# Layer 0's mixer stage in another order: the first products, the 64-row products of the recurrent mixer, and the additions of a sum of squares

## The chip, the cores and the metric

The kernel runs on one core of one Trainium2 chip. The metric is the device time of one execution in microseconds, median of several runs. A profiled execution gives the trace from which all rows below come.

## What is computed

A two-layer encoder trunk works on 1024 new frames of one stream and 64 frames of a running stream: 1088 columns in all (T), of model width 1024. Layer 0, the only one that the change touches, has two mixers behind one normalisation: a short gated convolution and a gated recurrent mixer (GLA) of four heads, 64 key and 128 value rows each. Per chunk of 64 frames:

```python
h = rms_norm(x, norm_mix[0])
... = split(h @ w_in_ab)
log_a = log_sigmoid(gk_low @ gk_w2 + gk_b) / 16
b = cumsum(log_a);  q_e = q * exp(b);  k_e = k * exp(-b)
att = where(causal, q_e @ k_e.T, 0)
o = att @ v + q_e @ S
S = exp(b_last) * S + (k * exp(b_last - b)).T @ v
o = rms_norm(o, onorm) * silu(g)
```

After it come the output projection with a residual and a SwiGLU FFN. Layer 1 is softmax attention over a band of chunks, with its own FFN.

## The kernel before

All activations stand transposed, features on the partitions and frames on the columns, in three column groups of 384, 384 and 320 (`GROUPS`, L24). Weights and activations are split into a high and a low part of a shorter float type (`hi`, `lo`), and each product is made of three: hi·hi, hi·lo, lo·hi (`chain`, L241). One `gemm` (L253) is three chains of 24 products, one for each group. The normalisation is not applied to the input: the sum of squares `RS` over the 1024 features goes through a product with ones, and 1/rms is multiplied in when a product leaves PSUM.

Layer 0's mixer stage, the first 415 us, is in this order:

- **First products** (L573 to L597). For each group and each of 8 row tiles: `hi` is the input times a gain (on ACT, or on DVE for odd tiles, L582), `lo` the rest (DVE, L585), the square is added into `RS[g]` by GpSimd (L590), and eight products go to three banks, `pg` (gate), `pk` (keys) and `pq` (queries) of the first pair of heads. Behind each group a `tail` (L557) is started, which makes 1/rms, the low-rank gate input `gkl` (L567), the exponentials of the gates (`gate_exps`, L370) and the scaled keys and queries.
- **v**, two GEMMs (L599, L600), whose results are turned to frames-on-partitions by `to_tokens` (L359).
- **The recurrent mixer** `gla_mix` (L447), beside the GEMMs of the output gate (`gla_gate`, L435) and of the second pair's k, q, v; then again for the second pair of heads beside the next gate GEMMs and the convolution's.

In `gla_mix` a pair of heads stands on the two halves of the 128 partitions. For each chunk a state product `kv` for each head takes 64 rows: the upper half for an even chunk, the lower half for an odd one. For each group and head there is then a score product `at` over 128-frame tiles (64 rows, those of the head), a mask on DVE, and an output product `po`: for each tile attention times v over 128 rows, then the two chunks' states over the head's 64 rows. A product with ones over its squares follows (`ss`, L510), for the norm.

TensorE's order is written by the kernel itself (`PEOrder`, L41): the main line issues GEMM products, each of which spends its modelled time, and side jobs (Python generators) are resumed when their time is due. `yield 2500.0` means that the job goes on 2500 ns of modelled TensorE time later. The other engines' order is a scheduler's. The places in question:

```python
                    mm(kv[:, hh * P:(hh + 1) * P], d["kd"][r, t, :], d["v"][hh][r, t, :], True, True)
...
                yield 1000.0
...
                    mm(at[0:w, i, 0:w], d["E2"][r, cols], d["E1"][r, cols], True, True)
...
                yield 2500.0
                po = gps.tile([P, 512], F32, name="ao")
                for i in range(ntl):
...
                nc.gpsimd.tensor_tensor(RS[g], RS[g], x, op=ALU.add)
```

ACT evaluates silu from one table of functions, and logarithm and exponential from another; an `ACT_TABLE_LOAD` stands in its order wherever the table changes. The two silus of a pair (L441) wait for the gate GEMMs.

Of the kernel before, what the change touches and what calls it, by code (L numbers as in the profile page):

```python
# [10 lines left out]
F32 = mybir.dt.float32  # L11
# [7 lines left out]
P = 128  # L19
# [112 lines left out]
def trunk_kernel(  # L132
# [60 lines left out]
    def mm(out, lhsT, rhs, start, stop):  # L193
        pe.matmul(out, lhsT, rhs, start=start, stop=stop)  # L194
        n = rhs.free_size()
        order.spend(max(214.0, n / 0.6) if lhsT.dtype == F32 else max(107.0, n / 2.4))
# [22 lines left out]
    def fetch():  # L219
        if wpos[0] == len(wlist):  # L220
            return
        src, nk = wlist[wpos[0]]
        wpos[0] += 1
        raw = wpool.tile([P, KT, P], F32, name="wraw", bufs=1)
        sp.dma_start(raw[:, 0:nk, :], src)
        hi = wpool.tile([P, KT, P], F32R, name="whi")
        lo = wpool.tile([P, KT, P], F32R, name="wlo")
        with tc.high_priority(offset=-100):
            act.copy(hi[:, 0:nk, :], raw[:, 0:nk, :])  # L229
            for a, b in ((0, nk),) if cur["sub"] is dve else ((0, nk // 2), (nk // 2, nk)):  # L230
                cur["sub"].tensor_tensor(lo[:, a:b, :], raw[:, a:b, :], hi[:, a:b, :].bitcast(F32), op=ALU.subtract)  # L231
        order.use("act", nk * P)
        order.use("dve" if cur["sub"] is dve else "pool", nk * P)
        wready.append((hi, lo))
# [6 lines left out]
    def chain(w, acts, g, evac):  # L241
        hi, lo = w
        c0, c1 = GROUPS[g]
        nk = len(acts)
        ps = mm_tile()
        v = ps[:, 0:c1 - c0]
        for k, (ah, al) in enumerate(acts):
            mm(v, hi[:, k, :], ah[:, c0:c1], k == 0, False)
            mm(v, hi[:, k, :], al[:, c0:c1], False, False)
            mm(v, lo[:, k, :], ah[:, c0:c1], False, k == nk - 1)  # L250
        evac(g, c0, c1, v)

    def gemm(acts, evac):  # L253

        w = next_weights()
        for g in range(len(GROUPS)):
            chain(w, acts, g, evac)
# [188 lines left out]

    def gla_mix(pr, d):  # L447

        S = None
        for g, (c0, c1) in enumerate(GROUPS):  # L450
            n = c1 - c0
            nch = n // CH
            ntl = (n + P - 1) // P
            states = []
            for cl in range(nch):
                c = c0 // CH + cl
                t, cc = c // 2, c % 2
                kv = gps.tile([P, 512], F32, name="kv")
                r = slice(cc * CH, (cc + 1) * CH)
                for hh in range(2):  # L460
                    mm(kv[:, hh * P:(hh + 1) * P], d["kd"][r, t, :], d["v"][hh][r, t, :], True, True)
                if c == TP // CH:
                    sp.dma_start(o_gla[0, pr], S)
                    S = G1.tile([P, P], F32, name="S", bufs=7)
                    sp.dma_start(S, glas[pr])
                states.append(S)
                Sn = G1.tile([P, P], F32, name="S", bufs=7)
                for hh in range(2):
                    r = slice(hh * CH, (hh + 1) * CH)
                    if S is None:  # L470
                        dve.tensor_copy(Sn[r, :], kv[r, hh * P:(hh + 1) * P])
                    else:
                        dve.scalar_tensor_tensor(Sn[r, :], S[r, :], d["E4"][r, c:c + 1],
                                                 kv[r, hh * P:(hh + 1) * P], op0=ALU.mult, op1=ALU.add)
                S = Sn
                yield 1000.0
            if g == 2:
                sp.dma_start(o_gla[1, pr], S)
            for hh in range(2):
                r = slice(hh * CH, (hh + 1) * CH)  # L480
                at = gps.tile([P, 4, P], F32, name="ao")
                for i in range(ntl):
                    w = min(P, n - i * P)
                    cols = slice(c0 + i * P, c0 + i * P + w)
                    mm(at[0:w, i, 0:w], d["E2"][r, cols], d["E1"][r, cols], True, True)
                am = attm[attc[0] % 2]
                attc[0] += 1
                full = n // P
                for i in range(full):
                    dve.copy_predicated(am[:, i, :], cmask, at[:, i, :])  # L490
                if n % P:
                    dve.copy_predicated(am[0:CH, full, 0:CH], cmask[0:CH, 0:CH], at[0:CH, full, 0:CH])
                yield 2500.0
                po = gps.tile([P, 512], F32, name="ao")
                for i in range(ntl):
                    w = min(P, n - i * P)
                    mm(po[:, i * P:i * P + w], d["v"][hh][:, 3 * g + i, :], am[:, i, 0:w], True, False)
                    for cc in range(w // CH):
                        st = states[2 * i + cc]
                        if st is None:  # L500
                            continue
                        k0 = i * P + cc * CH
                        mm(po[:, k0:k0 + CH], st[r, :], d["E1"][r, c0 + k0:c0 + k0 + CH],
                           False, cc == w // CH - 1)
                o_sb = gtmp()[:, 0:n]
                act.copy(o_sb, po[:, 0:n])
                sq = gtmp()[:, 0:n]
                act.activation(sq, o_sb, AF.Square)
                yield 3500.0
                ss = tr_tile()[:, 0:n]  # L510
                mm(ss, ones, sq, True, True)
                z = gtmp()[:, 0:n]
                rsqrt_newton(ss, n, float(P), z, sq, 1)
                dve.scalar_tensor_tensor(o_sb, o_sb, on, z, op0=ALU.mult, op1=ALU.mult)
                while not d["gate"]:
                    yield 1000.0
                dve.tensor_tensor(o_sb, o_sb, d["sg"][hh][:, c0:c1], op=ALU.mult)
                yh, yl = YB[2 * pr + hh]
                split(o_sb, yh[:, c0:c1], yl[:, c0:c1])
# [36 lines left out]

    def tail(g, c0, c1, pg, pk, pq):  # L557
        n = c1 - c0
        yield 3000.0
        ss = tr_tile()[:, 0:n]  # L560
        mm(ss, ones, RS[g], True, True)
        t = scratch()
        rsqrt_newton(ss, n, float(KT * P), RS[g], t[:, 0:n], 1)
        gl = gkl[:, c0:c1]
        act.copy(gl, pg[32:48, :])
        dve.tensor_tensor(gl, pg[0:16, :], gl, op=ALU.add)
        dve.tensor_tensor(gl, gl, RS[g][0:16, :], op=ALU.mult)  # L567
        yield 5800.0
        gate_exps(0, dd[0], g, c0, c1)
        ek(g, c0, c1, pk)  # L570
        eq(g, c0, c1, pq)

    for g, (c0, c1) in enumerate(GROUPS):  # L573
        n = c1 - c0
        pg, pk, pq = [t[:, 0:n] for t in (mm_tile(), gps.tile([P, 512], F32, name="kv"),
                                          gps.tile([P, 512], F32, name="ao"))]
        for k in range(KT):
            x = xs[k][:, c0:c1]
            hi, lo = xg[k][0][:, c0:c1], xg[k][1][:, c0:c1]
            gcol = gain[:, 0, k:k + 1]  # L580
            if k % 2:
                dve.tensor_scalar(hi, x, gcol, None, op0=ALU.mult)  # L582
            else:
                act.activation(hi, x, AF.Copy, scale=gcol)
            dve.scalar_tensor_tensor(lo, x, gcol, hi.bitcast(F32), op0=ALU.mult, op1=ALU.subtract)  # L585
            if k == 0:
                act.activation(RS[g], x, AF.Square)
            else:
                act.activation(x, x, AF.Square)
                nc.gpsimd.tensor_tensor(RS[g], RS[g], x, op=ALU.add)  # L590
            first, end = k == 0, k == KT - 1
            for ps, wh, wl in ((pg, gw, None), (pk, khi, klo), (pq, qhi, qlo)):
                mm(ps, wh[:, k, :], hi, first, False)
                mm(ps, wh[:, k, :], lo, False, end and wl is None)
                if wl is not None:
                    mm(ps, wl[:, k, :], hi, False, end)
        order.start(tail(g, c0, c1, pg, pk, pq))  # L597
    fetch()
    gemm(xg, ev0)  # L599
    gemm(xg, ev1)  # L600
    order.flush()
    zero_tails(dd[1])
    order.start(gla_mix(0, dd[0]))

    def gates1():
        for g, (c0, c1) in enumerate(GROUPS):
            gate_exps(1, dd[1], g, c0, c1)
            yield 3000.0

    order.start(gates1())  # L610
    gla_gate(dd[0])
# [614 lines left out]
```

## Time and profile before

| | |
|---|---|
| time, median of 3 runs | 2782.14 us (2781.51, 2791.0, 2782.14) |
| the profiled execution's own time | 2782.32 us |
| its span | 2780.6 us |
| mean granted clock of TensorE | 0.994 of full speed |
| busy: TensorE / DVE / ACT / GpSimd | 2708.6 / 1311.7 / 960.8 / 326.1 us |
| layer 0's mixer stage | 0 to about 415 us of the span |

The span is the profiled stretch of the program on the chip; the time holds 1.7 us more around it. PE is TensorE, PEld its weight loads, POOL GpSimd, SP the engine that issues transfers. A busy time is the time in which an instruction stood on the engine. Products on TensorE overlap in the records, so how long one takes is read from the distance of starts.

### The profile page before, as it was taken

To read this page: it belongs to the slowest core of one execution; us is meant where nothing else is said; L and a number is where in the kernel's file an instruction comes from. 1 tells how busy PE (TensorE), PEld (TensorE's weight loads), DVE (VectorE), ACT (ScalarE), POOL (GpSimd) and SP (SyncE) were. 2 spreads that over 40 slices of the span, in tenths; PEclk is the share of its full clock that TensorE was granted. 3 is DMA by queue.
4 is the path that set the end of the run, shared out by engine and by line. 5 is a ranking of instruction groups with operands and counts; after the bars stand their busy time and mean duration, and the time that the engine had idled before them with its cause. 6 is when DMAs were issued, how large, how long until landed. Compare 5 with 4: busy or idle time off the path is not lost.

```text
span 2780.6 us, 40392 instructions
## 1 busy us (share of the span) xinstructions
PE 2708.6 (97%) x16514; PEld 2634.7 (95%) x16514; DVE 1311.7 (47%) x2782; ACT 960.8 (35%) x1937; POOL 326.1 (12%) x382
## 2 busy tenths in 40 slices
PE   7999999999999999999999999989999999999999
PEld 6888999999999999999988888979899999999999
DVE  6554644433223323345677777775633323333332
ACT  4423213322112102234677777865522112111210
POOL 4000002000000000013433333341300000000000
PEclk9999999999999999999999999999999999999999
DMA  4101113111111111122111111143211111111112
GB/s 153 39 26 32 33 46 110 46 46 41 43 46 46 43 49 46 43 71 93 60 59 44 58 55 57 54 128 101 102 46 46 45 40 46 45 47 46 46 53 81
DMA packets 73736, 160.73 MB, mean 58 GB/s; under 512 B 11296, under 2 KB 44592, under 8 KB 73520
## 3 DMA queue, kind: packets, MB, share of 16 engines
q1 hardware_dynamic: 73552, 158.16, 17.7%
q8 instruction: 130, 2.13, 0.3%
q14 instruction: 54, 0.44, 0.1%
HBM read 136.98 MB, written 25.08 MB: 58 GB/s over the span
## 4 chain that ended last, share of the span: by engine, by line
PE 82%; ACT 7%; DVE 6%; issue 2%; DMA 2%; POOL 1%; SPq 0%; DVEq 0%; POOLq 0%; ACTq 0%
PE mm L194 75%; PE ao L194 2%; ACT s L903 2%; DVE s L899 1%; PE kv L194 1%; PE pt L199 1%; PE misc L194 1%; ACT ph L270 1%; PE S L194 1%; ACT s L907 1%; DVE pl L271 1%; DMA ta<-in_cv_dram 1%; DVE s L909 1%; ACT whi L229 1%; ACT qz L283 0%
## 5 line engine op out<-in xcount | busy, mean ns | idle before, releaser
L194 PE MATMUL mm<-a,whi 128*128 128x384 f32 (+1 forms) x5760 | 1454.8, 332 | 10.4 <-DVE x L676 5.1
L194 PEld LDWEIGHTS mm<-a,whi 128*128 128x128 f32 x5760 | 1020.4, 189 | 24.8 <-DVE x L676 7.8
L194 PE MATMUL mm<-a,wlo 128*128 128x384 f32 (+1 forms) x2880 | 952.0, 331 | 0.0
L194 PEld LDWEIGHTS mm<-a,wlo 128*128 128x128 f32 x2880 | 543.3, 189 | 5.6 <-issue 1.1
L229 ACT CAST whi<-wraw 128x1024 fp32r<-128x1024 f32 (+2 forms) x201 | 205.6, 1023 | 646.6 <-PE mm L194 641.3
L194 PE MATMUL mm<-bh,wlo 128*128 128x384 f32 (+1 forms) x1056 | 344.7, 326 | 0.0
L194 PE MATMUL mm<-bh,whi 128*128 128x384 f32 (+1 forms) x1056 | 344.4, 326 | 0.0
L194 PE MATMUL mm<-bl,whi 128*128 128x384 f32 (+1 forms) x1056 | 344.2, 326 | 0.0
L701 DVE TENSOR_TENSOR ts<-mm,rs 128x384 f32<-128x384 f32 x132 | 70.7, 535 | 349.2 <-PE mm L194 349.2
L231 DVE TENSOR_TENSOR wlo<-wraw,whi 128x1024 fp32r<-128x1024 f32 (+1 forms) x171 | 205.9, 1204 | 54.9 <-ACT whi L229 52.9
L279 POOL TENSOR_TENSOR rs<-rs,ta 128x384 f32<-128x384 f32 (+1 forms) x54 | 58.4, 1081 | 1225.3 <-ACT ta L278 1224.6
L194 PEld LDWEIGHTS mm<-bh,whi 128*128 128x128 f32 x1056 | 198.2, 188 | 0.2
L194 PEld LDWEIGHTS mm<-bl,whi 128*128 128x128 f32 x1056 | 198.2, 188 | 0.1
L194 PEld LDWEIGHTS mm<-bh,wlo 128*128 128x128 f32 x1056 | 198.2, 188 | 0.1
L707 DVE TENSOR_TENSOR ta<-mm,rs 128x384 f32<-128x384 f32 x132 | 70.7, 536 | 224.4 <-PE mm L194 224.4
L186 ACT ACTIVATE ts<-ts 128x384 f32<-128x384 f32 (+1 forms) x130 | 65.7, 505 | 294.8 <-DVE ts L701 294.8
L676 DVE TENSOR_TENSOR x<-x,mm 128x384 f32<-128x384 f32 (+1 forms) x96 | 50.6, 530 | 200.3 <-PE mm L194 193.4
L676 DVE TENSOR_TENSOR xr<-xr,mm 128x384 f32<-128x384 f32 (+1 forms) x96 | 51.1, 532 | 195.5 <-PE mm L194 192.8
L903 ACT ACTIVATE s<-s,mx 128x640 f32<-128x640 f32 (+4 forms) x144 | 101.6, 706 | 63.1 <-DVE mx L899 59.8
L199 PE MATMUL pt<-ident,s 128*128 128x128 f32 x560 | 93.2, 277 | 16.6 <-DVE pl L271 8.7
L271 DVE TENSOR_TENSOR pl<-pt,ph 128x384 fp32r<-128x384 f32 (+2 forms) x192 | 90.3, 486 | 36.6 <-ACT ph L270 35.7
L199 PEld LDWEIGHTS pt<-ident,s 128*128 128x128 f32 x560 | 68.5, 141 | 29.2 <-DVE pl L271 9.6
(256 smaller groups left out, 3712.6 us busy)
## 6 DMA issues: line engine op xcount, KB each, us to landing
wraw<-in_w_f_dram SPq DMA_DIRECT2D x104, 512.0 KB, 3.3
wraw<-in_w_f_dram SPq DMA_DIRECT2D x32, 448.0 KB, 3.3
wraw<-in_w_qkv_dram SPq DMA_DIRECT2D x24, 512.0 KB, 3.5
wraw<-in_w_in_dram SPq DMA_DIRECT2D x23, 512.0 KB, 3.6
B<-in_bias_dram SPq DMA_DIRECT2D x16, 320.0 KB, 3.0
xr<-in_xT_dram SPq DMA_DIRECT2D x8, 544.0 KB, 7.2
wraw<-in_w_out_dram SPq DMA_DIRECT2D x8, 512.0 KB, 3.5
a_sp<-ao SPq DMA_DIRECT2D x28, 128.0 KB, 1.7
```

Of the source, the lines that this page charges most:

```text
L186: cur["silu"] = act.activation(x, x, AF.Silu).ins
L194: pe.matmul(out, lhsT, rhs, start=start, stop=stop)
L199: pe.transpose(out, in_, idn)
L229: act.copy(hi[:, 0:nk, :], raw[:, 0:nk, :])
L231: cur["sub"].tensor_tensor(lo[:, a:b, :], raw[:, a:b, :], hi[:, a:b, :].bitcast(F32), op=ALU.subtract)
L270: act.copy(hi, x)
L271: sub.tensor_tensor(lo, x, hi.bitcast(F32), op=ALU.subtract)
L279: add.tensor_tensor(RS[g], RS[g], sq[:, 0:n], op=ALU.add)
L676: dve.tensor_tensor(xv, xv, ps, op=ALU.add)
L701: dve.tensor_tensor(s, ps, RS[g], op=ALU.mult)
L707: dve.tensor_tensor(u, ps, RS[g], op=ALU.mult)
L903: act.activation(s[rows, 0:nk], s[rows, 0:nk], AF.Exp, bias=mx[rows, 0:1], scale=-1.0, accum_out=mx[rows, 1:2])
```

## The change

Three things are rewritten in layer 0's mixer stage.

**The mixer.** The state products of a 128-row tile's two chunks are issued together, eight in a row. The score product of the next output is issued directly behind the present one (`attend`). In an output product all attention products come first, then all states. The waits between the pieces change with it.

**The first products.** Only every fourth tile's `hi` is made on DVE, the squares are added on DVE, the v chains of groups 0 and 1 go ahead of the first products of group 2, and the tails have other delays (1500 and 7500 for 3000 and 5800).

**The second pair's gates** start 5000 later and stand 5000 apart (before 3000); the first `gla_mix` starts 1500 later.

```diff
     def gla_mix(pr, d):
...
+        def attend(g, hh):
...
+            for i in range((n + P - 1) // P):
...
+                mm(at[0:w, i, 0:w], d["E2"][r, cols], d["E1"][r, cols], True, True)
...
-            for cl in range(nch):
-                c = c0 // CH + cl
-                t, cc = c // 2, c % 2
-                kv = gps.tile([P, 512], F32, name="kv")
-                r = slice(cc * CH, (cc + 1) * CH)
-                for hh in range(2):
-                    mm(kv[:, hh * P:(hh + 1) * P], d["kd"][r, t, :], d["v"][hh][r, t, :], True, True)
...
-                yield 1000.0
+            for i in range(ntl):
+                t = 3 * g + i
+                chunks = range(2 * t, min(2 * t + 2, c1 // CH))
+                kvs = []
+                for c in chunks:
+                    kv = gps.tile([P, 512], F32, name="kv")
+                    r = slice(c % 2 * CH, (c % 2 + 1) * CH)
+                    for hh in range(2):
+                        mm(kv[:, hh * P:(hh + 1) * P], d["kd"][r, t, :], d["v"][hh][r, t, :], True, True)
+                    kvs.append(kv)
...
+                yield 1700.0 * len(kvs)
...
+            if am is None:
+                am = attend(g, 0)
+                yield 2500.0
             for hh in range(2):
...
-                yield 2500.0
                 po = gps.tile([P, 512], F32, name="ao")
                 for i in range(ntl):
                     w = min(P, n - i * P)
-                    mm(po[:, i * P:i * P + w], d["v"][hh][:, 3 * g + i, :], am[:, i, 0:w], True, False)
-                    for cc in range(w // CH):
...
-                        mm(po[:, k0:k0 + CH], st[r, :], d["E1"][r, c0 + k0:c0 + k0 + CH],
-                           False, cc == w // CH - 1)
+                    mm(po[:, i * P:i * P + w], d["v"][hh][:, 3 * g + i, :], am[:, i, 0:w], i == 0, False)
+                for cl in range(nch):
+                    if states[cl] is not None:
+                        k0 = cl * CH
+                        mm(po[:, k0:k0 + CH], states[cl][r, :], d["E1"][r, c0 + k0:c0 + k0 + CH],
+                           False, cl == nch - 1)
+                if hh == 0:
+                    am = attend(g, 1)
+                elif g + 1 < len(GROUPS):
+                    am = attend(g + 1, 0)
...
     def tail(g, c0, c1, pg, pk, pq):
...
-        yield 3000.0
+        yield 1500.0
...
-        yield 5800.0
+        yield 7500.0
...
-            if k % 2:
+            if k % 4 == 3:
                 dve.tensor_scalar(hi, x, gcol, None, op0=ALU.mult)
...
-                nc.gpsimd.tensor_tensor(RS[g], RS[g], x, op=ALU.add)
+                dve.tensor_tensor(RS[g], RS[g], x, op=ALU.add)
...
+    first_products(0)
+    first_products(1)
+    wv = wready.pop(0)
+    chain(wv, xg, 0, ev0)
+    chain(wv, xg, 1, ev0)
+    first_products(2)
     fetch()
-    gemm(xg, ev0)
+    chain(wv, xg, 2, ev0)
+    fetch()
     gemm(xg, ev1)
     order.flush()
     zero_tails(dd[1])
-    order.start(gla_mix(0, dd[0]))
+    order.start(gla_mix(0, dd[0]), 1500.0)
 
     def gates1():
+        yield 5000.0
         for g, (c0, c1) in enumerate(GROUPS):
             gate_exps(1, dd[1], g, c0, c1)
-            yield 3000.0
+            yield 5000.0
```

How TensorE's order changes at group 0's state products of the first pair, in `gla_mix`, beside the first gate GEMM (`mm`: GEMM products; `kv<-v,kd`: state products of one head; `tr<-gkl`: the gate product of the second pair). Before:

```order
L194 MATMUL mm<-a_3_89,whi 128x384
L194 MATMUL kv<-v_150,kd 128x128
L194 MATMUL kv<-v_151,kd 128x128
L194 MATMUL mm<-a_2_88,wlo 128x384
L194 MATMUL mm<-a_4_90,whi 128x384
L194 MATMUL mm<-a_5_91,whi 128x384
L194 MATMUL mm<-a_4_90,wlo 128x384
L194 MATMUL kv<-v_150,kd 128x128
L194 MATMUL kv<-v_151,kd 128x128
```

With the change:

```order
L194 MATMUL mm<-a_6_92,whi 128x384
L194 MATMUL kv<-v_150,kd 128x128
L194 MATMUL kv<-v_151,kd 128x128
L194 MATMUL kv<-v_150,kd 128x128
L194 MATMUL kv<-v_151,kd 128x128
L194 MATMUL mm<-a_7_93,whi 128x384
```

The state products of an even and an odd chunk now follow each other, and with them one return to GEMM products is left out.

TensorE's order at the first output product (group 0, first head; `ao<-attm,v`: attention times v, `ao<-E,S`: queries times states, `ao<-E,E`: scores). Before:

```order
L194 MATMUL ao<-attm_140,v_150 128x128
L194 MATMUL ao<-E_145,S 128x64
L194 MATMUL ao<-attm_140,v_150 128x128
L194 MATMUL ao<-E_145,S 128x64 x2
L194 MATMUL ao<-attm_140,v_150 128x128
L194 MATMUL ao<-E_145,S 128x64 x2
```

With the change:

```order
L194 MATMUL mm<-a_11_97,whi 128x320
L194 MATMUL ao<-attm_140,v_150 128x128 x3
L194 MATMUL ao<-E_145,S 128x64 x5
L194 MATMUL ao<-E_145,E_146 128x128 x3
L194 MATMUL tr<-gkl,w_130 128x320
L194 MATMUL mm<-a_10_96,wlo 128x320
```

The six alternating pieces became two, and the second head's scores, which stood by themselves among GEMM products, stand directly behind the states.

ACT's order at the two silus of the first pair (`sg`; `E<-g`: exponentials of the second pair's gates, `g<-tr,epsc` and the two behind it: the norm of the first head's first output; `whi<-wraw`: weight casts). Before:

```order
L229 CAST whi<-wraw 128x1024
L186 ACT_TABLE_LOAD
L186 ACTIVATE sg_152<-sg_152 128x1088
L270 CAST yb0h_120<-g_987 128x384
L229 CAST whi<-wraw 128x1024
L186 ACTIVATE sg_153<-sg_153 128x1088
L176 ACT_TABLE_LOAD
L506 COPY g_1176<-ao 128x384
```

With the change, from the last of these exponentials, five rows behind the first silu, to the second silu:

```order
L389 ACTIVATE E_156<-g_1035 128x320
L390 ACTIVATE E_157<-g_1031 128x5
L283 ACT_TABLE_LOAD
L283 ACTIVATE g_1046<-tr,epsc 128x384
L284 ACT_TABLE_LOAD
L284 ACTIVATE g_1046<-g_1046 128x384
L285 ACTIVATE g_1020<-g_1046 128x384
L270 CAST yb0h_120<-g_1018 128x384
L229 CAST whi<-wraw 128x1024
L186 ACT_TABLE_LOAD
L186 ACTIVATE sg_153<-sg_153 128x1088
L176 ACT_TABLE_LOAD
```

Gate exponentials and the norm's steps now stand between the two silus, with a table load at each change: in the first mixer 6 loads for 2, in the second 5 for 2.

## Rows read from the trace of the kernel before

**Rows 1.** The page, part 1: busy us of each engine, share, instructions.

```profile
PE 2708.6 (97%) x16514; PEld 2634.7 (95%) x16514; DVE 1311.7 (47%) x2782; ACT 960.8 (35%) x1937; POOL 326.1 (12%) x382
```

**Rows 2.** TensorE's waits, 0 to 420 us: total, times, longest.

```profile
PE tr L194 <- DVE gkl L567: 7.2, 1, 7.2
PE tr L194 <- POOL rs L590: 3.7, 1, 3.7
```

**Rows 3.** By stretch: length, busy PE, PEld, DVE, ACT, POOL (times), clock, DMA, GB/s.

```profile
30.00:63.00 33.00, 25.33 (x119) 22.66 (x120) 17.72 (x29) 9.17 (x21) 13.88 (x15) 0.79 0.14 50
...
92.00:300.00 208.00, 206.72 (x1204) 179.78 (x1204) 107.01 (x243) 69.60 (x127) 0.00 (x0) 1.00 0.10 30
```

**Rows 4.** TensorE in order of time, first products: start, us, what.

```profile
23.17 0.51 PE L194 MATMUL mm<-a,yb0h 128*128 128x384 f32 x2
...
24.56 0.51 PE L194 MATMUL mm<-a,yb0h 128*128 128x384 f32 x2
...
63.05 0.51 PE L194 MATMUL mm<-a,whi 128*128 128x384 f32 x2
```

**Rows 5.** GpSimd's and DVE's order of time at the first products.

```profile
12.45 10.25 POOL L590 TENSOR_TENSOR rs<-rs,E 128x384 f32<-128x384 f32 x1 [10.15 <-ACT E L589]
22.78 1.01 POOL L590 TENSOR_TENSOR rs<-rs,kd 128x384 f32<-128x384 f32 x1
...
20.45 0.62 DVE L585 SCALAR_TENSOR_TENSOR a<-sg,gain,a 128x384 fp32r<-128x384 f32 x1
20.98 0.39 DVE L582 TENSOR_SCALAR a<-E,gain 128x320 fp32r<-128x320 f32 x1
...
32.98 1.13 DVE L582 TENSOR_SCALAR a<-sg,gain 128x320 fp32r<-128x320 f32 x1
```

**Rows 6.** TensorE's order of time: state products (kv) between GEMM products.

```profile
135.89 0.81 PE L194 MATMUL tr<-g,ones 128*128 128x384 f32 x2
136.63 0.72 PE L194 MATMUL kv<-v,kd 64*128 64x128 f32 x8
...
137.56 0.34 PE L194 MATMUL mm<-a,wlo 128*128 128x384 f32 x1
...
142.92 0.34 PE L194 MATMUL mm<-a,whi 128*128 128x384 f32 x1
143.19 0.71 PE L194 MATMUL kv<-v,kd 64*128 64x128 f32 x4
...
144.11 0.34 PE L194 MATMUL mm<-a,wlo 128*128 128x384 f32 x1
```

**Rows 7.** TensorE's order of time: an output product, then a score product.

```profile
131.02 0.38 PE L194 MATMUL ao<-attm,v 128*128 128x128 f32 x2
131.33 0.43 PE L194 MATMUL ao<-E,S 64*128 64x64 f32 x2
131.69 0.49 PE L194 MATMUL ao<-attm,v 128*128 128x128 f32 x2
132.11 0.66 PE L194 MATMUL ao<-E,S 64*128 64x64 f32 x4
132.70 0.49 PE L194 MATMUL ao<-attm,v 128*128 128x128 f32 x2
...
144.73 0.93 PE L194 MATMUL ao<-E,E 64*128 64x128 f32 x6
...
145.87 0.51 PE L194 MATMUL mm<-a,whi 128*128 128x384 f32 x2
```

**Rows 8.** ACT's order of time at the second silu.

```profile
127.73 1.04 ACT L229 CAST whi<-wraw 128x1024 fp32r<-128x1024 f32 x1 [7.24 <-PE mm L194]
128.68 1.11 ACT L186 ACTIVATE sg<-sg 128x1088 f32<-128x1088 f32 x1
129.81 1.28 ACT L176 ACT_TABLE_LOAD   x1
133.81 0.48 ACT L506 COPY g<-ao 128x384 f32<-128x384 f32 x1 [2.72 <-PE ao L194]
```

More of the change, by code (lines that the diff above doesn't have):

```diff
@@ L449, in gla_mix @@
         S = None
+        def attend(g, hh):
+            c0, c1 = GROUPS[g]
+            n = c1 - c0
+            r = slice(hh * CH, (hh + 1) * CH)
+            at = gps.tile([P, 4, P], F32, name="ao")
+            for i in range((n + P - 1) // P):
+                w = min(P, n - i * P)
+                cols = slice(c0 + i * P, c0 + i * P + w)
+                mm(at[0:w, i, 0:w], d["E2"][r, cols], d["E1"][r, cols], True, True)
+            am = attm[attc[0] % 2]
+            attc[0] += 1
+            full = n // P
+            for i in range(full):
+                dve.copy_predicated(am[:, i, :], cmask, at[:, i, :])
+            if n % P:
+                dve.copy_predicated(am[0:CH, full, 0:CH], cmask[0:CH, 0:CH], at[0:CH, full, 0:CH])
+            return am
+        am = None
         for g, (c0, c1) in enumerate(GROUPS):
@@ L454, in gla_mix @@
             states = []
-            for cl in range(nch):
-                c = c0 // CH + cl
-                t, cc = c // 2, c % 2
-                kv = gps.tile([P, 512], F32, name="kv")
-                r = slice(cc * CH, (cc + 1) * CH)
-                for hh in range(2):
-                    mm(kv[:, hh * P:(hh + 1) * P], d["kd"][r, t, :], d["v"][hh][r, t, :], True, True)
[L462 to L475, printed above, removed]
-                yield 1000.0
+            for i in range(ntl):
[8 more added lines that the diff above has]
+                    kvs.append(kv)
+                for c, kv in zip(chunks, kvs):
+                    if c == TP // CH:
+                        sp.dma_start(o_gla[0, pr], S)
+                        S = G1.tile([P, P], F32, name="S", bufs=7)
+                        sp.dma_start(S, glas[pr])
+                    states.append(S)
+                    Sn = G1.tile([P, P], F32, name="S", bufs=7)
+                    for hh in range(2):
+                        r = slice(hh * CH, (hh + 1) * CH)
+                        if S is None:
+                            dve.tensor_copy(Sn[r, :], kv[r, hh * P:(hh + 1) * P])
+                        else:
+                            dve.scalar_tensor_tensor(Sn[r, :], S[r, :], d["E4"][r, c:c + 1],
+                                                     kv[r, hh * P:(hh + 1) * P], op0=ALU.mult, op1=ALU.add)
+                    S = Sn
+                yield 1700.0 * len(kvs)
@@ L477, in gla_mix @@
             if g == 2:
                 sp.dma_start(o_gla[1, pr], S)
+            if am is None:
+                am = attend(g, 0)
+                yield 2500.0
             for hh in range(2):
                 r = slice(hh * CH, (hh + 1) * CH)
[L481 to L492, printed above, removed]
-                yield 2500.0
                 po = gps.tile([P, 512], F32, name="ao")
@@ L496, in gla_mix @@
                     w = min(P, n - i * P)
-                    mm(po[:, i * P:i * P + w], d["v"][hh][:, 3 * g + i, :], am[:, i, 0:w], True, False)
-                    for cc in range(w // CH):
[L499 to L502, printed above, removed]
-                        mm(po[:, k0:k0 + CH], st[r, :], d["E1"][r, c0 + k0:c0 + k0 + CH],
-                           False, cc == w // CH - 1)
+                    mm(po[:, i * P:i * P + w], d["v"][hh][:, 3 * g + i, :], am[:, i, 0:w], i == 0, False)
[8 more added lines that the diff above has]
+                    am = attend(g + 1, 0)
                 o_sb = gtmp()[:, 0:n]
@@ L571, in tail, with first_products @@
         eq(g, c0, c1, pq)
-    for g, (c0, c1) in enumerate(GROUPS):
+    def first_products(g):
+        c0, c1 = GROUPS[g]
         n = c1 - c0
```

## The prediction

> **What bounds the kernel now.** I read the page first: TensorE is busy for 97% of the span, and all other engines for less than half of it [rows 1]. So work taken from TensorE shortens the kernel by as much, wherever TensorE has no other wait, and a wait of TensorE costs its full length. Then the waits of TensorE in the first 420 us, the only stretch whose order the change moves. There are two long ones: 7.2 us for the first group's gate input and 3.7 us for the sum over its squares [rows 2]. Both go back to the sum of squares RS. The table by stretch shows what came after them: in the stretch from 30 to 63 us the granted clock was 0.79 of full speed [rows 3], so products after each wait ran at the lower level of the clock, 1.2 GHz, not at 2.4 GHz. Last I read TensorE's own order of time around the recurrent mixer, product by product [rows 6, 7], because there the engine is never idle and the cost is in how products follow one another.
>
> **The first products.** From the first product of group 1, at 23.17 us, to the first product of the v GEMM, at 63.05 us, 39.9 us pass. Eight products of 384 columns take 24.56 - 23.17 = 1.39 us at full clock [rows 4], 0.174 us each. The stretch holds 64 of them (11.1 us), 64 of 320 columns (9.3 us by columns) and five small products, which I bound by the 0.74 us between the starts at 135.89 and 136.63 [rows 6], at most 3.7 us. That is 24.1 us of work, so 15.8 us are lost: 10.9 us of waiting and 4.9 us of slow products.
> Why RS is late: POOL adds the squares. Its first add stands in the trace with 10.25 us, while DVE splits tile after tile, and the next with 1.0 us; in turn DVE's scaling of 320 columns grows from 0.39 us beside the long add to 1.13 us beside the short ones [rows 5]. The change gives the 21 adds to DVE and 6 of DVE's 12 scalings to ACT. No add of this kind on DVE is in the trace. It is bounded by the scaling above (0.39) and by the three-operand instruction of 384 columns, 0.62 us, of which 0.53 us pass to the next start [rows 5]; I take 0.53, as it has two full operands too. That is a term of DVE's load; in the sum it counts only where DVE gets late. Per group DVE then has 8 such splits, 7 adds and 2 scalings, 15 x 0.53 + 2 x 0.33 = 8.6 us, against 11.1 us of TensorE. The RS of group 0 is complete near 19 us, and its product stands 11 products after 23.17 us, at 25 us. The first gate product follows 55 products after 23.17 us, near 33.4 us; I make its input ready near 31.4. The three groups' tails (some ten DVE instructions each, by the code) lie between, and the two v chains put ahead of group 2 add 8.3 us of TensorE work that asks nothing of DVE but their exits. At the k transposes of group 0 and the gate product of group 1 the margin is about nothing. I gain 15.8 us and give 1.0 us back there.
>
> **The mixer.** 64-row products stand between 128-row ones. Four state products (two heads, two passes each) take, from their first start to the second GEMM product behind them, 144.11 - 143.19 = 0.92 us; eight, of two chunks in different halves of the rows, take 137.56 - 136.63 = 0.93 us [rows 6]. So the second four cost nothing: products of different halves run side by side. From the GEMM product ahead, 144.11 - 142.92 = 1.19 us pass, with two steps of 0.174 in it: a group costs 0.84 us. Of 34 groups of four (17 chunks, two mixers), 4 pairs already stand together, so there are 30 passes; the changed order has 16 pairs and 2 single ones, 18 passes. 12 x 0.84 = **10.1 us** gained.
> An output product of group 0 is three times attention (2 passes) then states (2, 4, 4 passes). The pieces take 0.31 and 0.36, then 0.42 and 0.59 us [rows 7]. Two more state passes cost 0.23, so one costs 0.11 and entering the states costs 0.59 - 0.44 = 0.14; the attention piece after a return is 0.20 above its two steps. So an alternation costs 0.34 us; the new order removes two from each of 12 outputs, **8.2 us**.
> A score product (6 passes) alone: from 144.11 to 145.87 pass 1.76 us with four GEMM steps in it, so it costs 1.06 us [rows 6, 7]. 10 of 12 now stand directly behind states, and read the other half of the rows. Nearest row: the eight state products, which ran as fast as four. So I take the scores as hidden behind the ten state passes: 10 x 1.06 = **10.6 us**. If they queue, only what stands around the six passes is saved, 1.06 less six passes of 0.11, or 0.4 us each: 4.0 us. Both stay in the range.
> The Trainium skill speaks against the first value: "TensorE: Matmul & The Clock Gate", Part 3, "What overlaps and what doesn't", says that matmuls start and end strictly in program order and that only weight loads are pulled ahead. By it the scores wait until the last state product has started, and the sum is 6.6 us smaller. Eight products in the time of four speak for the larger value.
> All this is on the path: from 92 to 300 us TensorE is busy for 206.7 of 208 us [rows 3].
>
> **What becomes late.** First, ACT's tables. A table load takes 1.28 us [rows 8]. The new order has 7 more of them, 4 in the first mixer, since the second pair's gate chain now begins 5 us later and the first output's normaliser stands between the two silus. The trace gives a weight cast of 0.95 us (127.73 to 128.68), a silu of 1.13 with its hand-over and, at 384 columns, a copy of 0.48 [rows 8]; the other steps are estimates from these by columns, and DVE's from its 0.53. From the end of the first gate GEMM ACT does: cast 0.95, load, silu 1.13, load, four exponentials 1.2, load, logarithm 0.6, load, exponential and square 1.1; then DVE six instructions, 3.2, and ACT a cast, 0.5. That is 13.8 us, where the second gate GEMM lasts 48 x 0.174 + 24 x 0.145 = 11.8. Then cast 0.95, load, silu, load, copy and square 1.05: ready at 19.5 us. TensorE asks for it at 11.8 + 0.35 (two products) + 2.1 (the output) + 1.4 (eight products) = 15.6 us, since the score product no longer stands 2.5 us ahead of the output. It waits 3.9 us (in the trace ACT stood idle for 2.7 us before that copy [rows 8]); DVE, held by the same chain, frees a GEMM bank 0.4 us late. A wait of 3.7 us was followed by a slow clock, so I add 2.0 us. In the second mixer the same sum has two fewer swaps in series: 1.9 us. Second, in each group the norm product follows its output after 2 to 9 GEMM products, where ACT needs copy and square, 1.05 us, and two hand-overs: three of each mixer's six wait 0.3 to 1.0 us, 2.7 us together. With the 1.0 us of the start: **11.9 us** lost.
>
> **Sum.** 15.8 + 10.1 + 8.2 + 10.6 - 11.9 = 32.8 us. The profiled execution took 2782.3 us, its span 1.7 less, and is 0.2 us above the median of the three runs. 2782.3 - 32.8 = **2749.5 us**. From 420 us on every engine's order is the same, so nothing is gained or lost there.
>
> **Rivals.** (B) Scores queue behind states: 2749.5 + 6.6 = 2756.1. For it: they stand behind ten passes, not four; against it [rows 6]. (C) None of the new waits appears, because silu and loads find gaps that I placed too late: 2737.6. Against: the load chain is fixed by ACT's order. (D) DVE takes POOL's place as the late engine: it gets 21 x 0.53 - 6 x 0.33 = 9.1 us more in a stretch where it is busy anyway; were TensorE to wait that long, with 4.9 us of slow products after it, 2763.5. For: margins of nothing at two places; against: DVE without POOL beside it does in 0.39 what took 1.13. (E) The change does not do what it says: if the drain belonged to each 64-row product and not to the pass, standing together would save nothing: 2782.3 - 15.8 + 11.9 = 2778.4. Against: [rows 6]. (F) Slower. Place: the 12 norm products behind the outputs, which now stand closer to them. If each of them waited 3.9 us for ACT and had 2.2 us of slow products after it, 73 us go, 62 more than the 10.9 in my sum: 2812. It decides from an average of 3.6 us each, (44.7 - 1.0) / 12. Against: ACT is busy for 35% of the span [rows 1], and away from the silus the step needs 1.05 us.
>
> **Chances.** Forecast 0.45, B 0.22, C 0.10, D 0.15, E 0.05, F 0.03. 0.5% is 13.9 us, about what a measurement of this kernel can tell from no change: faster means under 2768.4. A to D lie there, 0.92; E is the same, 0.05; F slower, 0.03. The range 2736 to 2764 reaches from C to D.
>
> **What would show it.** TensorE: no wait of over 2 us between 20 and 70 us, the first v product of group 0 near 36 us, a granted clock of 1.0 from 30 to 63 us; RS adds on DVE at 0.5 us and none on POOL; eight state products together at about 0.65 us to the next GEMM product; a score product right behind ten state passes adding under 0.2 us; one wait of 3 to 5 us for ACT's square at the second head's first output, some 17 us earlier than its old place at 136 us. The forecast is wrong if scores cost 0.6 us each behind the states (B), if TensorE waits for DVE in the first 75 us (D), or if many norm products wait for more than 1 us (towards F).

## The result, and the profile after

The changed kernel takes 2758.56 us (median of 4 runs, 2754.32 to 2759.0); before it was 2782.12 us in the same comparison. The ratio is 0.9905, interval [0.9882, 0.9927]: faster by 23.6 us, where I forecast 32.6 under the median, 2749.5 us. The range (2736 to 2764) holds it.

The profiled execution took 2754.32 us, span 2752.6, so it is 4 us below the other three runs. A mark that does not depend on what comes later shows the change itself: the first product of the output projection, behind which the order is the same in both kernels. The rows are TensorE's order of time, of the kernel before:

```profile
416.22 0.41 PE L194 MATMUL mm<-yb0h,whi 128*128 128x384 f32 x1 [0.68 <-DVE ts L662]
```

and of the changed kernel:

```profile
391.14 0.41 PE L194 MATMUL mm<-yb0h,whi 128*128 128x384 f32 x1 [0.68 <-DVE ts L691]
```

That is 25.1 us. The other 2.9 us of this execution's 28.0 came after 1340 us, in layer 1, where no order differs, and the other three runs lie 4 us higher; so I count them as the run's, not as the change's. I compare marks below, since they tell differences of a microsecond that the times do not.

The page's first part of the changed kernel answers to [rows 1]:

```profile
PE 2683.9 (98%) x16514; PEld 2619.9 (95%) x16514; DVE 1309.3 (48%) x2797; ACT 972.2 (35%) x1950; POOL 294.8 (11%) x361
```

TensorE's waits from 0 to 420 us answer to [rows 2]. Both old ones are gone, and two new kinds stand in their place (the third line below is an old one, 1.3 us in the kernel before):

```profile
PE tr L194 <- ACT g L526: 4.4, 2, 3.4
PE kv L194 <- DVE S L499: 3.3, 2, 2.0
PE tr L199 <- DVE ta L426: 1.0, 2, 0.7
```

The table by stretch (columns as in [rows 3]):

```profile
30.00:63.00 33.00, 32.91 (x198) 30.56 (x197) 24.79 (x52) 16.14 (x35) 0.00 (x0) 1.00 0.15 48
...
120.00:130.00 10.00, 9.49 (x53) 8.50 (x53) 8.46 (x21) 1.22 (x3) 0.00 (x0) 0.84 0.00 0
145.00:160.00 15.00, 14.20 (x84) 13.06 (x85) 7.91 (x21) 3.83 (x9) 0.00 (x0) 0.89 0.15 49
92.00:300.00 208.00, 198.81 (x1259) 183.62 (x1259) 107.30 (x245) 78.77 (x129) 0.00 (x0) 0.98 0.11 32
```

The first products are repaired: 32.9 of 33 us busy at full clock, where it was 25.3 at 0.79. The mixer got worse in another way: TensorE stands for 9.2 of the 208 us, before for 1.3, and the clock falls twice behind the new waits.

**The start.** TensorE's order of time, the last gate product before group 0's v chain, and that chain's first product:

```profile
32.83 0.91 PE L194 MATMUL tr<-gkl,w 16*128 16x384 f32 x2
...
35.52 0.51 PE L194 MATMUL mm<-a,whi 128*128 128x384 f32 x2
```

The gate product stands at 32.8 us without a wait (I had 33.4) and the v chain begins at 35.5 (I had 36). DVE's order of time shows a scaling and the new add, against [rows 5]:

```profile
10.85 0.41 DVE L601 TENSOR_SCALAR a<-v,gain 128x384 fp32r<-128x384 f32 x1
...
11.71 0.55 DVE L609 TENSOR_TENSOR rs<-rs,E 128x384 f32<-128x384 f32 x1
12.18 0.61 DVE L604 SCALAR_TENSOR_TENSOR a<-v,gain,a 128x384 fp32r<-128x384 f32 x1
```

An add takes 0.55 us, with 0.47 to the next start (I had 0.53). At the first product of the first gate GEMM the changed kernel is 16.0 us ahead (75.67 for 91.65).

**An output product with scores behind it.** TensorE's order of time at group 0's second output:

```profile
109.39 0.83 PE L194 MATMUL ao<-attm,v 128*128 128x128 f32 x6
110.15 0.99 PE L194 MATMUL ao<-E,S 64*128 64x64 f32 x7
110.87 0.37 PE L194 MATMUL ao<-E,E 64*128 64x128 f32 x1
110.98 0.27 PE L194 MATMUL ao<-E,S 64*128 64x64 f32 x1
...
111.31 0.49 PE L194 MATMUL ao<-E,E 64*128 64x128 f32 x3
111.73 0.44 PE L194 MATMUL mm<-a,wlo 128*128 128x384 f32 x1
```

All ten state passes stand ahead of the six scores in the program. The first score starts beside the seventh state pass, three run beside states, and three stand alone at 0.11 us each. So the scores are half hidden.

**The wait for ACT.** TensorE's order of time in front of that output's norm product, the second head's, and behind it:

```profile
113.06 0.34 PE L194 MATMUL mm<-a,whi 128*128 128x384 f32 x1
116.84 1.65 PE L194 MATMUL tr<-g,ones 128*128 128x384 f32 x2 [3.45 <-ACT g L526]
...
120.07 0.52 PE L194 MATMUL mm<-a,wlo 128*128 128x384 f32 x1
120.39 0.84 PE L194 MATMUL mm<-a,whi 128*128 128x384 f32 x2
```

and ACT's order of time over the same stretch:

```profile
110.56 0.51 ACT L270 CAST yb0h<-g 128x384 fp32r<-128x384 f32 x1 [3.19 <-DVE g L535]
110.98 1.04 ACT L229 CAST whi<-wraw 128x1024 fp32r<-128x1024 f32 x1
112.04 1.28 ACT L186 ACT_TABLE_LOAD   x1
113.34 1.11 ACT L186 ACTIVATE sg<-sg 128x1088 f32<-128x1088 f32 x1
114.46 1.28 ACT L176 ACT_TABLE_LOAD   x1
115.76 0.48 ACT L524 COPY g<-ao 128x384 f32<-128x384 f32 x1
116.27 0.52 ACT L526 ACTIVATE g<-g 128x384 f32<-128x384 f32 x1
```

This is the chain that I had laid out: cast, weight cast, load, silu, load, copy, square. It ends 3.45 us after TensorE is ready (I had 3.9). Behind it a GEMM product steps by 0.32 us, not 0.174: the lower level of the clock, 1.2 GHz.

**The wait for DVE**, which I had not forecast. TensorE's order of time:

```profile
143.05 0.71 PE L194 MATMUL kv<-v,kd 64*128 64x128 f32 x4
145.80 0.68 PE L194 MATMUL kv<-v,kd 64*128 64x128 f32 x4 [2.04 <-DVE S L499]
```

and DVE's:

```profile
143.25 0.33 DVE L499 SCALAR_TENSOR_TENSOR S<-S,E,kv 64x128 f32<-64x128 f32 x1
143.58 1.22 DVE L231 TENSOR_TENSOR wlo<-wraw,whi 128x1024 fp32r<-128x1024 f32 x1
144.72 0.55 DVE L291 TENSOR_TENSOR g<-g,g 128x384 f32<-128x384 f32 x1
145.30 0.35 DVE L499 SCALAR_TENSOR_TENSOR S<-S,E,kv 64x128 f32<-64x128 f32 x1
```

Eight state products fill both `kv` buffers at once. The next pair needs both back, and the last state update of the pair before stands on DVE behind a weight split and a norm step. In the kernel before, with the groups of four apart, TensorE waited for state updates for 0.2 us in all. Whether the pairing or the steps between the updates make the wait, these rows do not tell; norm_later and calm_kv below bear on it.

### The profile page after: what moved, and what is told of

Read it like the earlier page. It is cut to its first block, busy times and chain, and to the rows that moved or that the text cites. A ratio compares the mean times of both kernels' runs of the same rounds, so it can differ in the third digit from the quotient of the medians.

```text
span 2752.6 us, 40413 instructions
## 1 busy us (share of the span) xinstructions
PE 2683.9 (98%) x16514; PEld 2619.9 (95%) x16514; DVE 1309.3 (48%) x2797; ACT 972.2 (35%) x1950; POOL 294.8 (11%) x361
## 4 chain that ended last, share of the span: by engine, by line
PE 81%; ACT 8%; DVE 7%; issue 2%; DMA 2%; POOL 1%; SPq 0%; DVEq 0%; POOLq 0%; ACTq 0%
PE mm L194 75%; ACT s L932 2%; DVE s L928 1%; PE ao L194 1%; PE pt L199 1%; PE misc L194 1%; PE kv L194 1%; ACT ph L270 1%; ACT s L936 1%; DVE pl L271 1%; PE S L194 1%; ACT whi L229 1%; PE tr L194 1%; DVE s L938 1%; DMA ta<-in_cv_dram 1%
## 5 line engine op out<-in xcount | busy, mean ns | idle before, releaser
L270 ACT CAST a<-ta 128x384 fp32r<-128x384 f32 (+1 forms) x72 | 35.6, 496 | 173.6 <-DVE ta L737 170.1
```

The source lines that it names most:

```text
L270: act.copy(hi, x)
```

## The experiments

Two theories to start with. Theory W: each part gained about what its rows say, and some 16 us of the mixer's gain went to new waits and slow products behind them. The rivals of each run say where that could fail. The mark is the first product of the output projection, except where a run's text names another. Each mark is read from one trace of its kernel.

| kernel | time, us | ratio to before, interval | mark, us |
|---|---|---|---|
| before | 2782.1 to 2784.8 | | 416.22 |
| changed | 2758.56 | 0.9905 [0.9882, 0.9927] | 391.14 |
| start_only | 2766.2 | 0.9952 [0.9935, 0.9970] | 400.24 |
| mix_only | 2770.14 | 0.9959 [0.9945, 0.9973] | 404.73 |
| gates_back | 2754.86 | 0.9902 [0.9887, 0.9917] | 388.37 |
| norm_later | 2750.99 | 0.9894 [0.9878, 0.9911] | 383.15 |
| calm | 2741.34 | 0.9843 [0.9817, 0.9868] | 376.60 |
| calm_scores | 2749.23 | 0.9866 [0.9834, 0.9897] | 383.91 |
| calm_states | 2750.35 | 0.9874 [0.9849, 0.9899] | 386.17 |
| calm_kv | 2755.62 | 0.9892 [0.9865, 0.9918] | 389.18 |
| calm_mixed | 2738.4 | 0.9824 [0.9799, 0.9848] | 374.57 |
| calm_same | 2742.85 (one run) | | 377.63 |
| adds_pool | 2767.74 | 0.9931 [0.9908, 0.9955] | 403.11 |
| v_after | 2758.98 | 0.9895 [0.9870, 0.9920] | 391.61 |

**start_only.** Old `gla_mix` and gate delays, new first products.

> The new first products, v chains and tail delays with the mixer and the second pair's gates of before. The mark is the first product of the output projection (416.2 us before, 391.1 with the whole change). Theory W (each part gained about what its rows say; the mixer's gain was given back by new waits of TensorE for ACT and DVE and by slow products behind them): the start is worth 16 us by itself and the mixer is as before, so mark at 400 us, time 2766 us. Rival X (the start's gain depends on the new mixer, since the old mixer with the new start meets ACT and DVE later in their own work): mark at 404 us or later, a new wait of over 2 us after 75 us.

Mark 400.24, 16.0 us before the old one; every later stage has its old length to 0.02 us, which also shows how closely two traces agree there. The start adds to the rest; rival X falls.

**mix_only.** Old first products and tails, new `gla_mix` and gate delays.

> The first products of before, the new mixer and gate delays. Theory W: mark at 416.2 - 9 = 407 us, time 2773 us, with the same two kinds of waits as in the whole change (3 to 4 us for the squares at the second head's first output, 2 us and 1 us for the state updates on DVE). Rival Y (the waits come from the new start, whose work is still in ACT's and DVE's queues when the mixer begins): the waits vanish, mark at 400 us.

Mark 404.73. Of the 11.5 us, 2.5 are gained before the mixer begins (the wait for the sum is gone, and the one for `gkl` is 10.6 us); the mixer gives 9.0. The waits are the same, 4.4 us for ACT and 3.3 for DVE in TensorE's waits, so they belong to the mixer's own order, and rival Y falls.

The 2.5 us are no gain of the change, since this kernel's first products are those of before. GpSimd's first add shows a difference (its order of time):

```profile
12.31 1.22 POOL L608 TENSOR_TENSOR rs<-rs,E 128x384 f32<-128x384 f32 x1 [10.02 <-ACT E L607]
```

It took 1.22 us here and 10.25 us in the trace of before [rows 5], and TensorE waited nearly as long for the sum's results, 10.6 us for 10.9. So the start of the old order is not the same in two traces: against this one the new start gains 13.5 us, against that of before 16.0. What makes the difference was not tried.

**gates_back.**

```diff
     def gates1():
-        yield 5000.0
         for g, (c0, c1) in enumerate(GROUPS):
             gate_exps(1, dd[1], g, c0, c1)
-            yield 5000.0
+            yield 3000.0
```

> The whole change, only the second pair's gates start at once and stand 3000 apart, as before: the order then has two table loads at the first pair's silus, not six, and the norm of the first output no longer stands as a block between them. Theory W: the wait of 3.4 us for the squares goes (under 0.7 us) and with it the slow products of 113 to 123 us, together 6 us; mark at 385 us, time 6 us below the changed kernel's. Rival Z (the table loads are not what makes the squares late; DVE's part of the norm is): the wait stays over 2.5 us, mark at 390 to 391 us.

Half. The wait of 3.4 us is gone, only the one of 1.0 us in the second mixer is left, where the edit changes nothing. So the second pair's gate chain between the two silus, with its table loads, did make the squares late, and rival Z falls. The edit moves the loads and the chain's other steps together; what each is worth it does not tell. But the mark is 2.8 us earlier, not 6: the waits for state updates stay at 3.3 us, and a slow stretch now lies at 130 to 160 us (granted clock 0.88 and 0.89).

**norm_later.** `yield 3500.0` ahead of the norm's product becomes `yield 6000.0`.

> The whole change, only the norm's product follows its output after 6000 and not 3500 of modelled time, some 14 GEMM products later. Theory W: every wait for squares goes, the table loads stay; mark 5 to 7 us earlier, at 385 us, as norm and next state products no longer meet on DVE only in part: the waits for state updates stay (2 us and 1 us). Rival V (TensorE's wait only moves: the next output or mask is late instead): mark within 1 us of 391 us.

Mark 383.15, 8.0 us earlier. No wait for ACT is left, and those for state updates fall from 3.3 to 0.6 us, more than I expected. At the place that cost 2.0 us, the four updates of the pair ahead now stand together on DVE (its order of time), where norm steps and a weight split stood between them in the changed kernel:

```profile
143.70 1.49 DVE L499 SCALAR_TENSOR_TENSOR S<-S,E,kv 64x128 f32<-64x128 f32 x4 [0.66 <-PE kv L194]
```

The state products are paired in both, so the pairing alone does not make the wait. One new wait came, in the second mixer (TensorE's order of time):

```profile
260.45 0.32 PE L194 MATMUL ao<-E,S 64*128 64x64 f32 x1 [3.38 <-DMA S<-in_glas_dram]
```

The running stream's start state is loaded in the middle of the mixer, issued by SP, which had stood at two weight loads for 21.2 us until 254.6 us (SP's order of time):

```profile
233.40 21.20 SPq L225 DMA_DIRECT2D wraw<-in_w_in_dram  x2
```

So a part of rival V is right too. That the load's place makes this wait is tried in calm.

**calm.** The late norm, and that state loaded at the program's start:

```diff
-                        S = G1.tile([P, P], F32, name="S", bufs=7)
-                        sp.dma_start(S, glas[pr])
+                        S = run_s[pr]
```

> The change with the norm at 6000, and the running stream's start state loaded at the program's start into tiles of its own, not in the middle of the mixer. Theory W: the wait of 3.4 us for that load goes, with 1 to 2 us of slow products behind it; mark (first product of the output projection; 383.15 us with the late norm alone) at 378 us, no wait of TensorE over 1 us between 75 and 378 us, time 12 to 13 us below the changed kernel's, 2745 us. Rival V (a wait only moves): mark at 381 us or later.

Mark 376.60, 14.5 us before the changed kernel's, 0.4 of them from the start. The table by stretch of this kernel, against 198.81 us at 0.98 above:

```profile
92.00:300.00 208.00, 206.22 (x1343) 193.37 (x1343) 117.54 (x263) 81.84 (x135) 0.00 (x0) 1.00 0.11 35
```

So 14.1 us of what the mixer's order had won was lost in waits and slow products, and is to be had by two edits that take no product away and move only the norm's product and one load. The wait for the start state is gone. All six table loads of the first mixer are still there, and with the norm's product later they hold TensorE up no more.

**calm_scores, calm_states, calm_kv** undo the three pieces one at a time, where no wait of over 1 us blurs them: scores issued one to eight GEMM products later; attention and states alternating; the two chunks' state products 1700 apart.

> As calm, but the ten scores that stand directly behind states are issued one to eight GEMM products later. Theory H (half hidden: three of six passes ran beside the last states): a score behind states adds 0.35 us, one by itself 1.06, so 10 x 0.7: mark 7 us after calm's. Rival P (all hidden, as I predicted): 10.6 us. Rival Q (they queue, only a change of kind is saved): 4 us.

> As calm, but in each output attention and states alternate as before the change; scores still behind. Theory: 24 alternations at 0.34 us, mark 8.2 us after calm's. Rival (a return from states to attention costs only what a wait for the last state costs, 0.2 us or less): under 5 us.

> As calm, but the state products of a tile's two chunks are issued apart, 1700 after each other. Theory: 16 more passes of four at 0.84 us, less what happens to stand together: mark 10 to 13 us after calm's. Rival E (the cost belongs to each 64-row product, not to the pass): under 3 us.

The marks come 7.3, 9.6 and 12.6 us after calm's, of which 0.4, 0.3 and 0.25 arise in the start. So the scores' place is worth 6.9 us: theory H, and neither all hidden nor queued. The alternation is worth 9.2 us (8.2 forecast); by TensorE's starts 8.0 of it lie inside the outputs, and the other 1.2 are not traced to a place. Sixteen more groups of four state products by themselves cost 12.3 us, 0.77 each, so the 12 that the change saved are worth 9.2 (10.1 forecast). Rival E falls. With the groups apart, TensorE still waits 0.8 us for a state update, for 0.6 in calm: no sign here that pairing makes that wait.

**calm_mixed.** The scores' three products stand in turn with the last three states in the program.

> As calm, but the score products stand in turn with the last three states of the output ahead of them. In the trace a score started beside the state pass four places ahead of it in the order and no earlier. Theory A (a product of the other half may start up to four places ahead, so in turn all six score passes run beside states): the session of attention, ten state passes and scores falls from 2.45 to about 2.12 us, mark 3 us before calm's. Rival B (three score passes at the end always stand alone, for the result's bank or the exit): session and mark as in calm, within 0.7 us.

Theory A. TensorE's order of time at the same output:

```profile
110.24 0.54 PE L194 MATMUL ao<-E,S 64*128 64x64 f32 x3
110.52 0.37 PE L194 MATMUL ao<-E,E 64*128 64x128 f32 x1
110.62 0.27 PE L194 MATMUL ao<-E,S 64*128 64x64 f32 x1
...
111.18 0.27 PE L194 MATMUL ao<-E,E 64*128 64x128 f32 x1
111.18 0.38 PE L194 MATMUL ao<-E,S 64*128 64x64 f32 x2
111.50 0.62 PE L194 MATMUL mm<-a,whi 128*128 128x384 f32 x2
```

From the first state to the next GEMM product 1.26 us pass, where the changed kernel needs 111.73 - 110.15 = 1.58. In calm_scores the ten state passes alone take as long (TensorE's order of time):

```profile
112.36 1.33 PE L194 MATMUL ao<-E,S 64*128 64x64 f32 x10
113.62 0.62 PE L194 MATMUL mm<-a,whi 128*128 128x384 f32 x2
```

So at this output the scores cost nothing any more, and the same holds for six of the ten outputs with scores behind them. In the other four the scores belong to group 2, and the third score product has 64 columns of weights where all others have 128 (`64*64` in calm_mixed's rows):

```profile
136.38 0.61 PE L194 MATMUL ao<-E,S 64*128 64x64 f32 x4
136.91 0.33 PE L194 MATMUL ao<-E,E 64*64 64x64 f32 x2
```

Its two passes start only behind the last state, and such an output gains 0.10 us on calm, not 0.33. What keeps them there was not tried. The mark is 2.0 us earlier, 2.3 without the start (3 forecast), and this is the fastest kernel of the study.

**calm_same.** Group 1's heads in reversed order, so that 4 of 10 scores use the half that the states use.

> As calm, but group 1's heads are taken in reversed order, so the scores that stand behind group 0's second and group 1's second output read the same half of the rows as the states ahead of them (4 of the 10). Theory (only different halves run side by side): these four sessions have no interleaved rows and cost 0.3 us more each, mark 1.3 us after calm's. Rival (any 64-row product may run beside another): rows and mark as in calm.

TensorE's order of time at the same output, whose scores now read the half of the states:

```profile
110.09 1.32 PE L194 MATMUL ao<-E,S 64*128 64x64 f32 x10
111.25 0.88 PE L194 MATMUL ao<-E,E 64*128 64x128 f32 x6
112.06 0.62 PE L194 MATMUL mm<-a,whi 128*128 128x384 f32 x2
```

Ten, then six, with nothing between: 1.97 us. The mark is 1.0 us later than calm's, 1.2 without the start. So products of the same half do not run side by side, and those of different halves do.

**adds_pool and v_after** take the start apart.

> The whole change, only the squares are added on GpSimd again. The mark here is the first product of the first gate GEMM (91.65 us before, 75.67 with the change). Theory R (the late sum of squares was GpSimd's doing): a wait of TensorE of 3 us or more for rs or gkl returns, and slow products behind it: mark at 79 us or later. Rival K (the v chains ahead of group 2 are what covers it): mark within 1.5 us of 75.7.

> The whole change, only the v chains stand behind all first products as before the change; the squares are added on DVE. Theory R (the adds on DVE suffice): mark (first product of the first gate GEMM) within 1.5 us of 75.7. Rival K (the v chains are the cover for group 0's tail): TensorE waits 3 us or more for gkl, mark at 79 us or later.

With the adds on GpSimd the first gate GEMM begins at 87.45 us, 11.8 us later, and TensorE's waits show the old one, longer:

```profile
PE tr L194 <- DVE gkl L585: 8.6, 1, 8.6
```

The add of 10.25 us [rows 5] is not in this trace, the first takes 1.05 us; it was not needed for the harm, as in mix_only. GpSimd still needs 8 us for a group's seven adds, and DVE's scalings grow beside them (its order of time, a tile of 320 columns, for 0.41 at 384 above):

```profile
27.28 1.14 DVE L601 TENSOR_SCALAR a<-v,gain 128x320 fp32r<-128x320 f32 x1
```

With the v chains behind, the first gate GEMM begins at 74.91 us, 0.8 earlier than with the change, and the last mark is 0.5 later. So the adds on DVE carry 11.8 of the 16 us, the chains' new place none. How the other 4 divide between the scalings on ACT and the tails' delays was not tried; mix_only's trace, with the old start, shows 2.5 us less than that of before without any edit there, so as much of the 4 may not be the change's.

## Why the prediction was right or wrong

**Right in direction and in three of its five terms, 9 us too low.** Most of that is in the mark: I had 32.8 us by 420 us, and 25.1 came.

- **The start**, 15.8 less 1.0: measured 16.0. The bound by rows was right, and DVE was never late; rival D did not come. That GpSimd's adds make the sum late is shown by adds_pool. The first add of 10.25 us, which I put first among the reasons, is not needed: in mix_only, with the same first products, it took 1.22 us, and TensorE lost 10.6 us in the wait for `gkl`. That trace's start is 2.5 us shorter than the one I summed from, so the agreement of 15.8 and 16.0 is in part luck.
- **State products paired**, 10.1: measured 9.2. **Alternations**, 8.2: measured 9.2. Both prices were read from the trace of before and hold within 1 us.
- **Scores**, 10.6: measured 6.9. This step failed: "I take the scores as hidden behind the ten state passes". The row that I leaned on, eight state passes in the time of four, has four of one half ahead of four of the other; there every pass finds its partner four places ahead. Behind ten state passes only the first three of the six score passes found one, and each score cost 0.32 us. Rival B's 4.0 fell as well. The Trainium skill's rule that matmuls start in program order ("TensorE: Matmul & The Clock Gate", Part 3, "What overlaps and what doesn't") does not hold for these products: the score at 110.87 us started ahead of three state passes that stand before it in the program. The Trainium skill's page "TensorEngine Tiling (Array Packing)", Key Properties, says that different tiles execute matmuls in parallel, which the trace bears out, but not how far ahead.
- **New waits**, 10.9 in the mixers. Those for ACT were sized well in the first mixer (3.9, measured 3.45) and too high in the second (1.9, measured 1.0). The small waits of norm products (2.7) did not come. Instead state updates waited on DVE, 3.3 us, with a slow stretch after them, and that was named nowhere: I had looked for ACT behind the changed order and not at the norm steps that come to stand between a pair's state updates on DVE. norm_later takes 2.7 of the 3.3 us away. Pieces of 25.3 us (9.2 + 9.2 + 6.9) and 9.1 on the mark leave 16.2 us lost, against my 10.9; calm shows 14.1 of them as waits and slow products. The other 2 are not traced to a place.
- By this, 14.8 + 28.9 - 10.9 = 32.8 became 16.0 + 25.3 - 16.2 = 25.1.
- **The signs that I named**: full clock from 30 to 63 us, adds of 0.5 us on DVE, the v product near 36 us, eight state products at 0.65 us (123.51 to 124.16) and the wait of 3 to 5 us came. A score behind states adds 0.32 us (1.58 for 1.26), not under 0.2. TensorE waited for ACT at 113.1 us, further ahead of 136 than the 17 us I gave.

## What to carry to other kernels

Price a piece by the distance of starts, and then ask what each new neighbour demands of buffers and of the engine that frees them: here the mixer's pieces brought 25 us and took 16 back, of which 14 were regained by lengthening one delay and moving one load. A step that follows its input by a fixed delay should be set back when what lay between is removed. Two streams of half-height products should stand in turn in the program, a product or two of each; behind one another they meet only at the seam.

## What was not expected of the hardware

TensorE ran 64-row products of different halves of the rows side by side, each starting beside one that stands at most four places ahead of it in the program: the first score pass, eleventh of the 64-row passes there, at 110.87 us beside the seventh of ten state passes; six of six in turn (1.26 us for sixteen passes); none when both read the same half (1.97 us). A product with 64 columns of weights did not join those with 128 (136.91 us in calm_mixed). The first add on GpSimd of 128x384 took 10.25 us in the kernel before [rows 5], 1.22 us in mix_only with the same first products, and 1.05 us in adds_pool; what made the difference was not tried.
